# A decoder layer in split fp32: the convolution's sum in PSUM, its gelu behind the next unit's roundings, the residual spread, and the down projection in chunks of 4, 6, 6 and 6 pairs

## The chip, the cores and the metric

One core of one Trainium2 chip. The metric is the device time of one execution in microseconds (us), the median of several runs. The matmul engine (TensorE) is called PE here, VectorE DVE, ScalarE ACT, GpSimd POOL, and SyncE, which only issues transfers, SP.

## The reference, cut to what matters

One decoder layer over 512 positions with 2048 channels: a mixer of four attention groups, an output projection, a layer norm with a scaled residual, then the gated MLP with a causal convolution of width 3 on its gate half, and a second layer norm. The change touches the MLP and what stands around it; D_FF is 5632, that is 44 tiles of 128 (f = 0 to 43).

```python
def conv_ffn(x, w_up, conv_w, conv_b, w_down):
    S = x.shape[1]
    u, g = jnp.split(x @ w_up, 2, axis=-1)
    gp = jnp.pad(g, ((0, 0), (CONV_WIDTH - 1, 0), (0, 0)))
    gc = conv_b
    for tap in range(CONV_WIDTH):
        gc = gc + conv_w[tap] * gp[:, tap:tap + S]
    return (jax.nn.gelu(gc) * u) @ w_down
...
ffn = conv_ffn(h, ffn_w_up[l], ffn_conv_w[l], ffn_conv_b[l], ffn_w_down[l])
h = layer_norm(DEEPNORM_ALPHA * h + ffn, ln2_g[l], ln2_b[l])
```

## The kernel before, in words

**Products.** Every fp32 operand is split into a high part (rounded to the matmul's fp32r) and a low part (the rest), and a product is three matmuls. Both projections of the MLP are done with seven block products in place of eight. A *unit* is one such set of seven, 84 matmuls of 128x128 by 128x256. The up projection has two units for each f (u = 0, 1), in the order (f,0), (f,1); only the last four stand as (42,1), (43,1), (42,0), (43,0). The down projection has 42 units; they run in chunks of pairs of f tiles (CHUNKS), each chunk over the four column sets q, so that a unit is named (chunk, q, u). Behind them stands a plain part of 96 matmuls (L1230) for the last four pairs of the last column set, with the second layer norm behind it. Matmuls of up are on L963, of down on L1115.

**A unit's weights** are made one unit ahead by weight_operands (L909 to L943), called from next_unit. SP loads two tiles wr. ACT writes the negated raw weights into wl (L925) and the rounded ones into wh (L928). POOL's queue then adds the raw weights onto wl with an accumulating transfer (L926), which leaves the low part; so this transfer waits for ACT's L925. POOL forms four sums S (L934 to L937), and each is split into ws by ACT (L899) and DVE (L900). wh and wl have two buffers each, wr four tiles (two units), S two. The first three block products of a unit use wh and wl, the other four ws.

**What stands behind an f.** When both units of f are done, up_finish reads its four PSUM banks (L995 to L1002), and gated makes the convolution: ACT's first tap into the SBUF tile c (L1010), DVE's other two taps (L1011, L1013), ACT's gelu (L1015), POOL's product with the up half (L1016). Every second f, set_aside forms differences of the pair on POOL (L1031, L1032, L1035, L1036) and writes eight blocks to DRAM (hid). up_residual scales the residual on DVE (L1054, L1055) for f = 2 to 17, one of 16 tiles behind each, from a load that it issues itself.

**Down.** hidden_operands loads a pair's blocks from DRAM (hx, hxt) and splits them on ACT and DVE; pairs 0 to 3 are called for in the middle of the last units of up, pairs 4 and 5 at the first unit of down, later ones six pairs ahead, in the last column set of a chunk, as its slots come free. down_add adds a finished set's seven banks into acc (L1128) and down_blocks ends a column set; the banks are those of up (three of group g, five of group a).

**What sets the order.** The code is recorded in program order, and a scheduler places each instruction by data dependence and by priority: weight_operands runs at a priority 900 places ahead, so that its rows move up past the work that stands before it in the code; splits of pairs below SLOTS run 10 ahead and later pairs' 150 behind. Each engine then runs its own row strictly in order.

## Time and profile before

| | us |
|---|---|
| median of 3 runs (lowest, highest) | 2334.61 (2327.23, 2335.04) |
| the profiled execution | 2341.35 |
| its span, first to last instruction | 2339.6 |
| PE busy | 2232.7 (95%) |
| granted clock of PE, mean | 0.983 |

The span has a mixer (to about 900 us), the up projection (917.56 to 1829.44 on PE without its first f), the down projection's units (1829.44 to 2291.86), and the plain part with the layer norm (to 2339.58). In the profile, a row of a timeline gives start, duration, engine, line, operation, result<-operands, count, and in brackets how long the engine had been idle before it and what ended that. A row of waits gives the sum of such idle times, how many, and the longest. The granted clock is 1.00 where TensorE runs at 2.4 GHz and 0.5 where it runs at 1.2 GHz.

### The profile page before, as it was taken

The page shows a single profiled execution, that of the slowest core. Times are in us where ns is not written, and L with a number is a line of the kernel's source. Part 1 is how long each engine was busy: PE and PEld are TensorE (multiplying, and loading weights), DVE is VectorE, ACT ScalarE, POOL GpSimd, SP SyncE. Part 2 cuts the span into 40 slices and gives each one's busy share as a digit, 9 for nine tenths or more (in the row PEclk, how much of TensorE's full clock was granted, in tenths as well). Part 3 has the DMA queues.
Part 4 walks back from the last instruction along what each step waited for, and adds up shares of the span by engine and source line. Part 5 has one row for each costly group of instructions (what it writes and reads, how often), then busy time and mean ns, then how long its engine had stood idle before and what let it go on. Part 6 is the DMA issues. An engine that isn't in the chain of part 4 may idle for free. (4 is left out here: it accounts for less than half of the span.)

```text
span 2339.6 us, 40306 instructions
## 1 busy us (share of the span) xinstructions
PE 2232.7 (95%) x15454; PEld 2083.5 (89%) x15454; DVE 1591.7 (68%) x2204; ACT 1229.5 (53%) x2129; POOL 1368.4 (58%) x1197
## 2 busy tenths in 40 slices
PE   7999999999999998899999999999999899999995
PEld 6788888888888878899999999999999899899994
DVE  7544455456675348687787767777676878677778
ACT  5444453355563135565555555565555666565651
POOL 5212110123234517787887878877777687777874
PEclk9999999999999999999999999999999999999998
DMA  6322223222124363888888777777778888788873
GB/s 228 92 81 73 78 67 106 84 64 62 59 88 149 104 188 94 224 226 227 231 222 238 202 210 207 201 204 197 212 202 227 243 241 233 193 229 216 207 191 115
DMA packets 125362, 392.75 MB, mean 168 GB/s; under 512 B 13632, under 2 KB 23744, under 8 KB 125168
## 3 DMA queue, kind: packets, MB, share of 16 engines
q1 hardware_dynamic: 106304, 287.72, 35.6%
q0 software_dynamic: 18720, 102.24, 24.6%
q8 instruction: 121, 1.98, 0.3%
q14 instruction: 73, 0.60, 0.1%
q10 hardware_dynamic: 144, 0.21, 0.0%
HBM read 354.36 MB, written 35.65 MB: 167 GB/s over the span
## 5 line engine op out<-in xcount | busy, mean ns | idle before, releaser
L900 DVE TENSOR_TENSOR ws<-S,ws 128x512 fp32r<-128x512 f32 x512 | 600.1, 1192 | 244.3 <-ACT ws L899 238.9
L963 PE MATMUL up<-xt,ws 128*128 128x256 f32 x3096 | 386.4, 283 | 0.3 <-DVE ws L900 0.3
L963 PEld LDWEIGHTS up<-xt,ws 128*128 128x128 f32 x3096 | 378.0, 192 | 0.6 <-DVE ws L900 0.6
L899 ACT CAST ws<-S 128x512 fp32r<-128x512 f32 x512 | 307.0, 615 | 114.9 <-POOL S L934 33.5
L100 DVE TENSOR_TENSOR wl<-wr,wh 128x1024 fp32r<-128x1024 f32 x122 | 155.2, 1272 | 213.3 <-ACT wh L99 198.4
L936 POOL TENSOR_TENSOR S<-wr 128x512 f32<-128x512 f32 x128 | 212.0, 1656 | 92.5 <-DVE ws L900 87.3
L342 POOL TENSOR_SCALAR P<-P,r 128x128 f32<-128x128 f32 (+3 forms) x144 | 81.1, 582 | 308.5 <-DVE r L337 166.2
L963 PE MATMUL up<-x,wh 128*128 128x256 f32 x1376 | 258.8, 288 | 0.0
L99 ACT CAST wh<-wr 128x1024 fp32r<-128x1024 f32 x122 | 128.0, 1049 | 233.7 <-PE op L733 78.8
L934 POOL TENSOR_TENSOR S<-wr 128x512 f32<-128x512 f32 x128 | 183.8, 1436 | 108.0 <-issue 45.3
L925 ACT ACTIVATE wl<-wr 128x512 fp32r<-128x512 f32 (+1 forms) x260 | 205.1, 836 | 67.3 <-PE dn L1115 43.5
L928 ACT CAST wh<-wr 128x512 fp32r<-128x512 f32 (+1 forms) x260 | 211.5, 829 | 35.7 <-PE up L963 33.8
L963 PE MATMUL up<-x,wl 128*128 128x256 f32 x688 | 200.8, 292 | 29.5 <-DMA wl<-in_wup_dram 29.3
L963 PEld LDWEIGHTS up<-x,wh 128*128 128x128 f32 x1376 | 220.5, 197 | 0.0
L937 POOL TENSOR_TENSOR S<-wr,S 128x512 f32<-128x512 f32 x128 | 211.8, 1655 | 0.0
L935 POOL TENSOR_TENSOR S<-S,wr 128x512 f32<-128x512 f32 x128 | 198.5, 1551 | 9.7
L1115 PE MATMUL dn<-wh,hx 128*128 128x256 f32 x792 | 157.5, 292 | 13.3 <-DVE acc L1128 8.6
L963 PEld LDWEIGHTS up<-x,wl 128*128 128x128 f32 x688 | 135.8, 197 | 33.7 <-DMA wl<-in_wup_dram 33.7
L1115 PEld LDWEIGHTS dn<-wh,hx 128*128 128x128 f32 x792 | 132.3, 200 | 14.9 <-issue 6.3
L733 PE MATMUL op<-wh,oTs 128*128 128x512 f32 x448 | 140.6, 391 | 0.0
L963 PE MATMUL up<-x,ws 128*128 128x256 f32 x1032 | 137.9, 283 | 0.0
L1015 ACT ACTIVATE c<-c 128x512 f32<-128x512 f32 x44 | 27.8, 632 | 208.0 <-DVE c L1013 208.0
(327 smaller groups left out, 5321.3 us busy)
## 6 DMA issues: line engine op xcount, KB each, us to landing
wr<-in_wup_dram SPq DMA_DIRECT2D x176, 512.0 KB
wl<-in_wup_dram POOLq DMA_DIRECT2D x88, 768.0 KB, 7.5
wr<-in_wm_dram SPq DMA_DIRECT2D x84, 512.0 KB
wr<-in_wdown_dram SPq DMA_DIRECT2D x84, 512.0 KB
wl<-in_wdown_dram POOLq DMA_DIRECT2D x42, 768.0 KB, 7.4
wr<-in_wout_dram SPq DMA_DIRECT2D x32, 512.0 KB
hid<-c SPq DMA_DIRECT2D x44, 256.0 KB
hid<-ht SPq DMA_DIRECT2D x44, 256.0 KB
```

The source lines that it names most:

```text
L100: nc.vector.tensor_sub(l[:, :cols], raw[:, :cols], h[:, :cols].bitcast(F32))
L733: nc.tensor.matmul(ps, ot[ct][:, a, t * P:(t + 1) * P], w[b][:, c2 * 512:(c2 + 1) * 512], start=(first and (a, b) == (0, 0)), stop=(last a ...
L899: self.nc.scalar.copy(h, raw)
L900: self.nc.vector.tensor_sub(l, raw, h.bitcast(F32))
L925: nc.scalar.mul(l3[:, o], i, -1.0)
L928: nc.scalar.copy(h3[:, o], i)
L934: nc.gpsimd.tensor_add(s12[:, 0], a21, a22)
L935: nc.gpsimd.tensor_sub(s12[:, 1], s12[:, 0], a11)
L936: nc.gpsimd.tensor_sub(s34[:, 0], a11, a21)
L937: nc.gpsimd.tensor_sub(s34[:, 1], a12, s12[:, 1])
L963: self.nc.tensor.matmul(ps, w[iw][i][:, k * P:(k + 1) * P], x[j][ix], start=(opens and k == 0 and (i, j) == (0, 0)), stop=(last and k == 3 ...
L1115: self.nc.tensor.matmul(bk[i][:, a * 256:(a + 1) * 256], x[ix][j][:, a * P:(a + 1) * P], w[iw][p][:, q * 256:(q + 1) * 256], start=first a ...
```

## The change

- **Convolution.** For f = 1 to 41 the sum c of the taps is kept in the PSUM bank bk[0] of the same f (its up product has been read by then); gelu reads that bank and writes an SBUF tile c. f = 0, 42 and 43 keep an SBUF tile.
- **Gelu later.** The gelu, the product with the up half and set_aside of f = 1 to 41 are put into a list (defer) and recorded when the next unit's weights have been recorded, and the scheduler is told to place them behind the last ACT row of those weights (issue_after, mark).
- **Residual.** One tile at f = 2, 4, ... 32 in place of f = 2 to 17, with the load one tile ahead of its use.
- **Border.** The splits of pairs 0 to 3 are deferred in the same way, by 0, 1, 1 and 2 units; pairs 4 and 5 are called for at unit (0,1,0).
- **Chunks** of 4, 6, 6, 6 pairs in place of 6, 6, 6, 4, all four column sets each, but the last set of the last chunk has one unit. The count of units, of matmuls and of weight loads is as before. There is one set of down_add more (16 for 15). The load of acc is issued at the first unit of a set of chunk 0, and that of the plain part's weights at unit (3,3,0).

```diff
     def split_pair(self, raw, h, l):
-        self.nc.scalar.copy(h, raw)
+        ins = self.nc.scalar.copy(h, raw)
         self.nc.vector.tensor_sub(l, raw, h.bitcast(F32))
+        return ins
+
+    def defer(self, units, work):
+        self.deferred.append((self.unit_no + units, work))
+
+    def run_deferred(self):
+        todo = [w for n, w in self.deferred if n < self.unit_no]
+        self.deferred = [d for d in self.deferred if d[0] >= self.unit_no]
+        with self.tc.issue_after(self.mark.ins):
+            for work in todo:
+                work()
...
         self.unit_no += 1
+        self.run_deferred()
...
-        self.gated(f, g, up)
+        self.gated(f, g, up, bk[0] if f < FT - 2 else None)
...
-        nc.scalar.activation(c, c, AF.Gelu_apprx_tanh)
+        if 0 < f < FT - 2:
+            self.defer(0, lambda: self.activate(f, c, up))
+        else:
+            self.activate(f, c, up)
+
+    def activate(self, f, s, up):
+        nc = self.nc
+        c = self.tmp("c") if 0 < f < FT - 2 else s
+        nc.scalar.activation(c, s, AF.Gelu_apprx_tanh)
         (nc.vector if f == 0 else nc.gpsimd).tensor_mul(c, c, up)
...
-    CHUNKS = ((0, 0, 6), (1, 6, 6), (2, 12, 6), (3, 18, 4))
+    CHUNKS = ((0, 0, 4), (1, 4, 6), (2, 10, 6), (3, 16, 6))
...
+        def split():
+            with self.tc.high_priority(offset=ahead):
+                for raw, h, l in loaded:
+                    self.split_pair(raw, h, l)
+
+        if kp < 4:
+            self.defer((0, 1, 1, 2)[kp], split)
+        else:
+            split()
...
-            if n and 2 <= f < 18:
-                self.up_residual(f - 2)
+            if n and 2 <= f < 34 and f % 2 == 0:
+                self.up_residual(f // 2 - 1)
```

ACT's row behind f = 27, before. c is the convolution's sum, wl and wh belong to unit (29,0), ws to (28,1) and (29,0), pu to f = 28.

```order
L928 CAST wh<-wr 128x1024
L899 CAST ws<-S 128x512 x3
L1010 ACTIVATE c<-g,prm 128x512
L1015 ACTIVATE c<-c 128x512
L928 CAST wh<-wr 128x512
L925 ACTIVATE wl<-wr 128x512
L925 ACTIVATE wl<-wr 128x1024
L899 CAST ws<-S 128x512
L928 CAST wh<-wr 128x1024
L899 CAST ws<-S 128x512 x3
L995 COPY pu<-up 128x256
```

The same place now; up in L1026 and L1039 is the PSUM bank.

```order
L942 CAST wh<-wr 128x1024
L899 CAST ws<-S 128x512 x3
L1026 ACTIVATE up<-g,prm 128x512
L942 CAST wh<-wr 128x512
L939 ACTIVATE wl<-wr 128x512
L939 ACTIVATE wl<-wr 128x1024
L899 CAST ws<-S 128x512
L942 CAST wh<-wr 128x1024
L899 CAST ws<-S 128x512
L1039 ACTIVATE c<-up 128x512
L899 CAST ws<-S 128x512 x2
L1009 COPY pu<-up 128x256
```

The gelu has moved from ahead of the next unit's negations (L925, now L939) to behind six rows of weights.

POOL's row at the same place, before: from the difference that needs only the first of the pair to the next unit's first sum.

```order
L1031 TENSOR_TENSOR ht<-c 128x256
L934 TENSOR_TENSOR S<-wr 128x512
L935 TENSOR_TENSOR S<-S,wr 128x512
L1016 TENSOR_TENSOR c<-c,up 128x512
L1032 TENSOR_TENSOR ht<-c,ht 128x256
L1035 TENSOR_TENSOR ht<-c 128x256
L1036 TENSOR_TENSOR ht<-c,ht 128x256
L926 DMA wl<-in_wup_dram 128x1536
L936 TENSOR_TENSOR S<-wr 128x512
L937 TENSOR_TENSOR S<-wr,S 128x512
```

And now:

```order
L948 TENSOR_TENSOR S<-wr 128x512
L949 TENSOR_TENSOR S<-S,wr 128x512
L940 DMA wl<-in_wup_dram 128x1536
L1055 TENSOR_TENSOR ht<-c 128x256
L1040 TENSOR_TENSOR c<-c,up 128x512
L950 TENSOR_TENSOR S<-wr 128x512
L951 TENSOR_TENSOR S<-wr,S 128x512
L1056 TENSOR_TENSOR ht<-c,ht 128x256
L1059 TENSOR_TENSOR ht<-c 128x256
L1060 TENSOR_TENSOR ht<-c,ht 128x256
```

The accumulating transfer of wl has moved ahead of the product with the up half and of three differences.

DVE's row at the border of up and down, before: from f = 42's reads of its banks (first L996) to f = 43's (second L996); hxt and hx are operands of the first pairs of down, ws those of units (0,0,0) and (0,0,1).

```order
L996 TENSOR_TENSOR pu<-pu,up 128x256
L997 TENSOR_TENSOR g<-pu,up 128x256
L998 TENSOR_TENSOR uu<-pu,up 128x512
L999 TENSOR_TENSOR g<-uu,up 128x256
L1001 TENSOR_TENSOR up<-uu,up 128x256
L1002 TENSOR_TENSOR up<-uu,up 128x256
L900 TENSOR_TENSOR ws<-S,ws 128x512 x2
L1011 SCALAR_TENSOR_TENSOR c<-g,prm,c 128x511
L900 TENSOR_TENSOR ws<-S,ws 128x512
L1013 SCALAR_TENSOR_TENSOR c<-g,prm,c 128x510
L900 TENSOR_TENSOR ws<-S,ws 128x512
L996 TENSOR_TENSOR pu<-pu,up 128x256
```

And now, from the row behind f = 42's last read to f = 43's first:

```order
L900 TENSOR_TENSOR ws<-S,ws 128x512 x2
L900 TENSOR_TENSOR hx<-hx 128x256 x2
L900 TENSOR_TENSOR ws<-S,ws 128x512
L900 TENSOR_TENSOR hxt<-hxt 128x512
L1027 SCALAR_TENSOR_TENSOR c<-g,prm,c 128x511
L900 TENSOR_TENSOR ws<-S,ws 128x512
L900 TENSOR_TENSOR hx<-hx 128x512 x2
L1029 SCALAR_TENSOR_TENSOR c<-g,prm,c 128x510
L900 TENSOR_TENSOR hx<-hx 128x512 x2
L900 TENSOR_TENSOR hxt<-hxt 128x512
L1010 TENSOR_TENSOR pu<-pu,up 128x256
```

Eight splits of pairs 1 and 2 now stand between the two. Before, splits of the first pairs stood ahead of f = 42's reads; now only pair 0's do.

## Rows read from the trace of the kernel before

**Rows 1.** The page's first part: busy time, share of the span and instructions of each engine.

```profile
PE 2232.7 (95%) x15454; PEld 2083.5 (89%) x15454; DVE 1591.7 (68%) x2204; ACT 1229.5 (53%) x2129; POOL 1368.4 (58%) x1197
```

**Rows 2.** PE's waits from 900 to 2340 us: what PE's line waited for, us in total, times, longest.

```profile
PE up L963 <- DMA wl<-in_wup_dram: 29.3, 20, 5.6
PE dn L1115 <- DVE acc L1128: 9.2, 4, 3.7
PE dn L1115 <- DMA wl<-in_wdown_dram: 8.2, 5, 2.1
```

**Rows 3.** Stretches of the span: from:to, its length, PE busy (matmul records), granted clock of PE, share of the DMA engines in use, GB/s. They begin with unit (2,0); unit (2,1); unit (42,0); units (0,0,0), (1,0,0), (2,0,0) and (3,0,0) of down; the plain part.

```profile
939.07:957.60 18.53, 12.60 (x86) 0.82 0.82 214
957.60:1803.08 845.48, 826.10 (x6807) 0.99 0.81 215
1803.08:1829.44 26.36, 21.86 (x170) 0.94 0.96 283
1829.44:1964.72 135.28, 126.85 (x1011) 0.96 0.88 241
1964.72:2096.53 131.81, 124.59 (x1010) 0.96 0.80 208
2096.53:2224.47 127.94, 123.09 (x1010) 0.99 0.82 216
2224.47:2291.86 67.39, 63.26 (x506) 0.97 0.70 182
2291.86:2339.58 47.72, 21.95 (x98) 0.76 0.28 102
```

**Rows 4.** PE's timeline: the first matmuls of units (28,0) and (28,1), and the one of (29,0) that waited.

```profile
1493.15 0.40 PE L963 MATMUL up<-x,wh 128*128 128x256 f32 x2
...
1503.23 0.40 PE L963 MATMUL up<-x,wh 128*128 128x256 f32 x2
...
1515.57 0.38 PE L963 MATMUL up<-x,wl 128*128 128x256 f32 x1 [1.87 <-DMA wl<-in_wup_dram]
```

**Rows 5.** PE's waits from 957.6 to 1803 us, where unit (2,1) begins and (42,0) begins.

```profile
PE up L963 <- DMA wl<-in_wup_dram: 19.3, 18, 4.5
```

**Rows 6.** ACT's timeline behind f = 27 (first tap, gelu, negations for unit (29,0), last ws splits).

```profile
1498.06 0.82 ACT L1010 ACTIVATE c<-g,prm 128x512 f32<-128x512 f32 x1 [4.17 <-DVE g L999]
1502.73 0.63 ACT L1015 ACTIVATE c<-c 128x512 f32<-128x512 f32 x1 [3.85 <-DVE c L1013]
...
1503.77 1.57 ACT L925 ACTIVATE wl<-wr 128x512 fp32r<-128x512 f32 x2
...
1506.71 1.66 ACT L899 CAST ws<-S 128x512 fp32r<-128x512 f32 x3
```

**Rows 7.** POOL's timeline at the same place.

```profile
1500.47 1.62 POOL L935 TENSOR_TENSOR S<-S,wr 128x512 f32<-128x512 f32 x1
1503.44 1.30 POOL L1016 TENSOR_TENSOR c<-c,up 128x512 f32<-128x512 f32 x1 [1.35 <-ACT c L1015]
...
1507.34 0.86 POOL L926 DMA_DIRECT2D wl<-in_wup_dram  x1
```

**Rows 8.** Groups of ACT's instructions from 957 to 1803 us: count, busy us, mean ns of one, idle time just before them and what ended it.

```profile
L1015 ACT ACTIVATE c<-c 128x512 f32<-128x512 f32 x41 | 25.9, 632 | 205.2 <-DVE c L1013 205.2
```

**Rows 9.** Groups of DVE's instructions, the first from 957 to 1803 us (one of the convolution's taps on DVE), the other two from 1830 to 2292 us (dn is a PSUM bank, pc its copy in SBUF).

```profile
L1011 DVE SCALAR_TENSOR_TENSOR c<-g,prm,c 128x511 f32<-128x511 f32 x40 | 67.3, 1681 | 0.0
...
L1128 DVE TENSOR_TENSOR acc<-acc,dn 128x512 f32<-128x512 f32 x82 | 53.3, 679 | 13.9 <-POOL acc L1128 9.2 <-DMA acc<-ares 3.0 <-PE dn L1115 1.5
L1128 DVE TENSOR_TENSOR acc<-acc,pc 128x512 f32<-128x512 f32 x28 | 43.4, 1549 | 0.0
```

**Rows 10.** Transfers issued from 957 to 1803 us: result<-source, queue, count, KB each, median us from issue to landing.

```profile
wl<-in_wup_dram POOLq DMA_DIRECT2D x81, 768.0 KB, 7.3
```

**Rows 11.** The border: POOL's issue for unit (42,0), PE's waits in (42,0), (0,0,0) and (0,0,2), and DVE's row that opens f = 42's reads.

```profile
1796.81 0.87 POOL L926 DMA_DIRECT2D wl<-in_wup_dram  x1
...
1807.98 0.58 PE L963 MATMUL up<-x,wl 128*128 128x256 f32 x1 [4.50 <-DMA wl<-in_wup_dram]
1833.25 0.39 PE L1115 MATMUL dn<-wh,hx 128*128 128x256 f32 x1 [2.20 <-DVE g L997]
1858.68 0.39 PE L1115 MATMUL dn<-wh,hx 128*128 128x256 f32 x1 [1.76 <-ACT hx L899]
...
1829.34 3.19 DVE L900 TENSOR_TENSOR hx<-hx 128x512 fp32r<-128x512 f32 x2
1832.46 0.41 DVE L996 TENSOR_TENSOR pu<-pu,up 128x256 f32<-128x256 f32 x1
```

**Rows 12.** Around the change from chunk 0's pairs to chunk 1's: PE at the start and in the first products of unit (1,1,0), and ACT before it.

```profile
2000.53 0.55 PE L1115 MATMUL dn<-wh,hx 128*128 128x256 f32 x1 [3.73 <-DVE acc L1128]
2003.15 0.58 PE L1115 MATMUL dn<-wl,hx 128*128 128x256 f32 x1 [2.06 <-DMA wl<-in_wdown_dram]
...
1996.64 0.62 ACT L899 CAST hx<-hx 128x512 fp32r<-128x512 f32 x1 [6.59 <-DMA hx<-hid]
```

**Rows 13.** The end of down: PE at unit (3,2,0), ACT at the plain part's weights, DVE's first row of the plain part.

```profile
2272.14 0.58 PE L1115 MATMUL dn<-wh,hx 128*128 128x256 f32 x1 [2.91 <-DVE acc L1128]
...
2269.55 1.14 ACT L113 CAST wres<-wr 128x512 fp32r<-128x512 f32 x2 [10.87 <-DMA wr<-in_wtail_dram]
...
2303.32 0.67 DVE L1233 TENSOR_TENSOR acc<-acc,dt 128x512 f32<-128x512 f32 x1
```

More of the change, by code (lines that the diff above doesn't have):

```diff
@@ L63, in __init__ @@
         self.every, self.count = 24, 0
-        self.late = deque()
+        self.late, self.deferred = deque(), []
         self.ahead = 0
@@ L773, in out_proj @@
                                    + [self.wdown[q, u] for c, k0, nk in self.CHUNKS
-                                      for q in self.column_sets(c)
-                                      for u in range(k0 // 2, (k0 + nk) // 2)])
+                                      for q in range(4)
+                                      for u in self.set_units(c, q, k0, nk)])
                 self.next_unit()
@@ L930, in weight_operands @@
                 w = [self.tmp("w21", dt=F32R, tag="w") for _ in range(2)]
-                self.split_pair(a21, *w)
+                self.mark = self.split_pair(a21, *w)
                 return [[h3[:, i], l3[:, i]] for i in range(3)] + [w]
@@ L941, in weight_operands @@
                     ws.append([self.tmp("ws", dt=F32R, tag="w") for _ in range(2)])
-                    self.split_pair(t[:, i], *ws[-1])
+                    self.mark = self.split_pair(t[:, i], *ws[-1])
         return [[h3[:, i], l3[:, i]] for i in range(3)] + ws
@@ L1002, in up_finish, with gated @@
         nc.vector.tensor_add(up[:, 256:], uu[:, 1], bk[2][:, :256])
-        self.gated(f, g, up)
-    def gated(self, f, g, up):
+        self.gated(f, g, up, bk[0] if f < FT - 2 else None)
+    def gated(self, f, g, up, c=None):
         nc = self.nc
-        c = self.tmp("c")
+        if c is None:
+            c = self.tmp("c")
         cw = lambda k: self.prm[:, C_CW + 44 * k + f:C_CW + 44 * k + f + 1]
@@ L1048, in up_residual, with load @@
         nc = self.nc
+        def load(i):
+            n, t = divmod(i, NT)
+            gb = (self.bc_row(2, n, "g1"), self.bc_row(3, n, "b1")) if t == 0 else None
+            a = self.tmp("res")
+            nc.sync.dma_start(a, self.res[t][n])
+            return a, gb
         n, t = divmod(i, NT)
-        if t == 0:
-            self.gb1 = self.bc_row(2, n, "g1"), self.bc_row(3, n, "b1")
-        a = self.tmp("res")
-        nc.sync.dma_start(a, self.res[t][n])
+        a, gb = self.res_next if i else load(i)
+        self.gb1 = gb or self.gb1
         nc.vector.scalar_tensor_tensor(a, a, ALPHA, self.gb1[0], op0=ALU.mult, op1=ALU.mult)
@@ L1057, in up_residual, with set_units @@
         nc.sync.dma_start(self.res[t][n], a)
-    CHUNKS = ((0, 0, 6), (1, 6, 6), (2, 12, 6), (3, 18, 4))
+        if i + 1 < 4 * NT:
+            self.res_next = load(i + 1)
+    CHUNKS = ((0, 0, 4), (1, 4, 6), (2, 10, 6), (3, 16, 6))
     @staticmethod
-    def column_sets(c):
-        return range(4 if c < 3 else 3)
+    def set_units(c, q, k0, nk):
+        return range(k0 // 2, (k0 + nk) // 2 if (c, q) != (3, 3) else k0 // 2 + 1)
     SLOTS = 6
@@ L1078, in hidden_operands @@
         loaded = []
-        ahead = 10 if kp < self.SLOTS else -150
+        ahead = 10 if kp < 4 else -150
         def load(h, l, src):
@@ L1105, in hidden_operands @@
             ops += [[h[:, k] for h in xt[i]] for k in range(2)]
-        with self.tc.high_priority(offset=ahead):
-            for raw, h, l in loaded:
-                self.split_pair(raw, h, l)
         self.ho[kp] = ops + b12
+        def split():
[6 more added lines that the diff above has]
+            split()
     def down_product(self, bk, w, i, q, x, first, last):
@@ L1180, in ffn @@
                 self.gated(f, *self.up_first())
-            if n and 2 <= f < 18:
-                self.up_residual(f - 2)
+            if n and 2 <= f < 34 and f % 2 == 0:
+                self.up_residual(f // 2 - 1)
         self.st2 = [self.cst.tile([P, 4, 6], F32, name=f"st2_{t}") for t in range(NT)]
-        self.due = deque((4, 5))
+        self.due = deque()
         acc = []
@@ L1187, in ffn @@
         for c, k0, nk in self.CHUNKS:
-            sets = self.column_sets(c)
-            for q in sets:
+            for q in range(4):
                 bk = [self.bank("g" if i < 3 else "a", "dn") for i in range(7)]
-                nu = nk // 2
+                nu = len(self.set_units(c, q, k0, nk))
                 for u in range(nu):
@@ L1194, in ffn @@
                     self.step_aside()
-                    if c == 0 and u == nu - 1:
+                    if c == 0 and u == 0:
                         acc.append([self.pT.tile([P, 2, 512], F32, tag="T", name="acc")
@@ L1200, in ffn @@
                             nc.sync.dma_start(token(t, q)[:, :cols], self.res[t][q][:, :cols])
+                    if (c, q, u) == (0, 1, 0):
+                        self.due.extend((4, 5))
+                    if (c, q) == (3, 3):
+                        tail = [w for f in range(2) for w in self.load_halves(self.wtail[f])]
                     while self.due:
@@ L1208, in ffn @@
                             self.down_add(i, acc[q], bk[i], c == 0)
-                    if q == sets[-1]:
+                    if q == 3:
                         for kp in (k0 + 2 * u, k0 + 2 * u + 1):
@@ L1213, in ffn @@
                                 self.due.append(kp)
-                        if c == 3 and u == 0:
-                            tail = [w for f in range(2) for w in self.load_halves(self.wtail[f])]
-                if c == 3 or (c, q) == (2, 3):
+                if c == 3:
                     self.down_blocks(q, acc[q])
```

## The prediction

> **What bounds the kernel now.** The page's first part shows PE busy for 95% of the span [rows 1], so only the rest of PE's time, and what a slower granted clock costs behind a wait, can be won. I then read PE's waits: three lines carry most of them, the accumulating transfer of wl in up with 29.3 us, banks that DVE's L1128 hands back late with 9.2, and the same transfer in down with 8.2 [rows 2]. The stretches tell where. A unit that waits for nothing takes 10.08 us (1493.15 to 1503.23) [rows 4], so each stretch has its count of units times 10.08, and an excess [rows 3]: up from (2,1) on, 81 units, 845.48 - 816.48 = 29.0; (42,0) and (43,0) 26.36 - 20.16 = 6.2; chunk 0 of down, 12 units, 135.28 - 120.96 = 14.3; chunk 1 10.85; chunk 2 7.0; chunk 3, 6 units, 6.9. Unit (2,0) has 8.45, at a place that the change leaves as it is. Of up's 29.0, 19.3 are 18 waits for the transfer, none over 4.5 [rows 5]; the rest is the clock, granted at 0.99 over this stretch [rows 3], so about 1% of 845.
>
> How a wait in up comes about is seen behind f = 27. ACT makes the first tap at 1498.06, then its queue stands at the gelu, 3.85 us idle for DVE's taps; the negations for unit (29,0) come behind it, to 1505.3 [rows 6]. POOL stands likewise at the product with the up half, makes three differences, and issues the transfer at 1507.34 [rows 7]. PE takes the result at 1515.57, 1.87 late [rows 4]: 8.2 us from issue, beside a median of 7.3 [rows 10].
>
> **Convolution, gelu, and the residual: up.** What is removed from the path is ACT's idle time before the gelu (205.2 us in 41 times, 5.0 each) and the gelu itself, 0.63 [rows 8], and on POOL the product, 1.30, and three differences, which fill 1504.7 to 1507.3 [rows 7]. The order shows the negations right behind the first tap and the transfer right behind the sum that ended at 1502.1 [rows 7]. The first tap ends at 1498.9; a rounding and negations of 1.57 behind it end near 1501 [rows 6], so the sum decides: issue at 1502.1 in place of 1507.34, 5.2 us earlier. With 8.2 us to landing wl is there at 1510.4, and PE wants it at 1513.7. Since no wait was longer than 4.5, all 18 go. I leave 3 of the 29.0 for transfers that land later than usual; the bounds are 0 (nothing late) and 12 (18 waits shortened by 5.2 only in part, because SP's loads go on sharing the DMA engines, busy 0.81 of this stretch [rows 3]). **Gain 26, from 17 to 29.**
>
> The taps in PSUM change DVE's time, not PE's. The taps on SBUF operands take 1.68 us; the trace has no such tap with its sum in PSUM. Nearest are adds of the same size, 0.68 with one operand in a bank and 1.55 with the copy in SBUF [rows 9]. I take 0.7 to 1.0 each, from 0.68 to 1.7 as bounds: DVE gets some 40 x 2 x 0.8 = 64 us back, beside PE, worth 0 by itself. The residual's 16 tiles have the same instructions; loaded one ahead, DVE no longer stands for them. That work lies beside PE's units; without that cover its two operations, priced like the taps at 0.7 to 1.7 each [rows 9], would be 1.4 to 3.4 a tile.
>
> The landing of 7.3 to 8.2 us is the number on which this hangs [rows 4, 7, 10]. The Trainium skill (DMA: Bandwidth & Descriptors, section Anatomy of one DMA — SWDGE (gpsimd) path) gives 2.0 us and bytes / 436e3 for such a transfer, an estimate of 3.8 us for 768 KB. By that, wl issued at 1507.34 would have landed ahead of PE, up and (42,0) would have had no wait, and 32.2 of the sum would fall away: 2323 in place of 2291. The trace does not agree (8.2), and the measurement decides.
>
> **Border of up and down.** Unit (42,0) waited 4.50 for a transfer issued at 1796.81 [rows 11], 11.2 before it arrived, behind the same gelu and differences of f = 41. Issued 5 us earlier it is in time even at 11.2: 6.2 goes to 0 (0 to 4 stays). In chunk 0 PE waits for f = 42's banks, which DVE reads only from 1832.46, after splits of the first pairs (3.19 for two of them), and at (0,0,2) for ACT's split of an operand [rows 11]. Now f = 42's reads stand ahead of the splits of pairs 1 to 3, so the first wait goes. New is that pair 1's splits stand behind four ws splits and a tap, and pair 1 is wanted within a microsecond of (0,0,0)'s start, at 1829.44; and that pair 3's are ordered in the same way at (0,0,1). Counting DVE's rows of the order from f = 42's reads at 0.7 to 1.6 each, pair 1 is ready 2 to 4 us late. Two such waits of 3, and as much again for the clock behind them as half their length: 9 in place of 14.3. Bounds: 3 (DVE gets there in time) and 18 (both 6 late). The same splits queue ahead of f = 43's bank reads, which (0,0,0) wants for its sixth product; a start 3 late covers that. The loads of hx stay where they were on SP, and acc's loads come earlier, with a whole set's time to spare. **Gain 6.2 + 5.3 = 11.5, from -1.5 to 17.5.**
>
> **Chunks.** The two changes of chunk with six pairs to exchange cost what chunks 1 and 2 have in excess, 10.85 and 7.0: ACT's row reaches a split whose load is still behind SP's weight loads (6.59 us), so ws and wl come late, and the bank of the next set too [rows 12]. The change with four pairs lies in chunk 3 and costs at most the 4.0 that its 6.9 has beside the wait of 2.91 [rows 3, 13]. Now again two changes have six pairs, one stretch later each, and one has four, two pairs being called for earlier at leisure. So I expect 18 for the two of six pairs, as before, and nothing new for the one of four: **gain 0, from -11 to 5** (each of six pairs at 14.5, or at 6.5). One more set of down_add is six adds of 0.68 and two of 1.55 on DVE [rows 9], 7.2 us, in a stage where DVE has room beside PE: 0.
>
> **End.** At (3,2,0) PE waited 2.91 because ACT had stood 10.87 for the plain part's weights, with a bank's copy behind them [rows 13]. Those loads now belong to (3,3,0), the last unit, so nothing but the plain part waits for them: chunk 3's 6.9 becomes 3.4 (0.5 to 7). DVE reached the plain part's first add at 2303.32, 11.5 us after the last of down's units, since the statistics of column set 2 and its blocks stood there [rows 3, 13]. They now fall a unit earlier; four statistics of 0.6 to 0.7 make 2.5 (0 to 4). **Gain 6, from 0 to 10.**
>
> **The sum.** 26 + 11.5 + 0 + 6 = 43.5. The profiled execution took 2341.35 (its span 2339.6 and 1.8 around it), so 2297.9 for it. It lies 6.7 above the median of the runs, so 2334.61 - 43.5 = **2291**.
>
> **The rivals.**
> (a) *Down gives back what up gains.* Border at 15, the changes of chunk at 29, chunk 3 at 5: 26 + 6.2 - 0.7 - 11 + 2 + 2.5 = 25, **2310**. For it: ACT stands 6.59 at a split already [rows 12], and the late splits go ahead of nothing but are wanted at once. Against it: most of the order of the six-pair changes is the same as before.
> (b) *The earlier transfer lands no earlier.* It would run beside SP's two loads for a unit, and the DMA engines are busy 0.81 [rows 3]. Then up keeps about half, 15 of 29, and (42,0) 3: 14 + 3.2 + 5.3 + 6 = 28.5, **2306**. Against it: the median of 7.3 holds at the same load [rows 10]. The Trainium skill (DMA: Bandwidth & Descriptors, section Issuing engines are not separate DMA queues) says that transfers of SP and POOL run on the same DMA engines and interleave; it speaks for this rival, and the (42,0) row, 11.2 us beside SP's extra loads, agrees with it [rows 11].
> (c) *Slower: the bank is held.* bk[0] of f is now free only after the gelu, and f + 2 writes it with its first product, 20.16 us after f's last matmul. The gelu stands behind ws splits that ended 15.2 us after f's last matmul with 5 us of idle ahead of them (1508.4 - 1493.15) [rows 4, 6], so I expect it at 11 to 12. It decides from 20.2 us on: each microsecond beyond is paid by 41 f. Two late on each are 82, **2373**; it is slower than before from some 1.1 late. Against it are those 8 us of slack.
> (d) *It doesn't do what it says:* the gelu is recorded later but reaches ACT's row in the old place. The order excludes that for the place; what can still be is that the transfer waits for the sum L935 of a later time. That is (b)'s time.
>
> **How the numbers follow.** Forecast, 2279 to 2303: 0.55. More than that, below 2279 (border near 3, up near 0): 0.07. (a) 0.18, (b) 0.12, (a) and (b) together, about 2324, 0.03, (c) 0.05. A difference within 0.5%, 11.7 us, is about what a measurement here can't tell from none; it is the range 2323 to 2346. A quarter of (a) and (b) and all of their sum fall there: 0.10. Slower is (c): 0.05. Faster is the rest, 0.85. The range 2277 to 2314 leaves out (c), the sum of (a) and (b), the tail of (a), and the lowest few per cent.
>
> **What would show it.** Right, if PE's wait for wl in up falls from 19.3 to under 5 and POOL issues the transfer near 9 us after the last f's end in place of 14; if ACT's idle time before the gelu falls from 205 to under 40; if the two taps take under 1 us each; if no PE wait in up names the gelu; if (0,0,0) and (0,0,1) wait for splits (hx) rather than for bank reads; if chunks 1 and 2 still have excesses of 7 to 11 with hx and acc as their names. Wrong, if wl is still waited for at odd f, if PE waits for the gelu, or if a change of chunk costs over 15.

## The result and the profile after

| | before | changed |
|---|---|---|
| median of 4 runs each, us (lowest, highest) | 2333.44 (2327.23, 2335.04) | 2306.91 (2301.35, 2309.40) |
| ratio, 95% interval | | 0.988 (0.986 to 0.990) |
| profiled execution, us | 2341.35 | 2307.26 |
| its span, us | 2339.6 | 2305.2 |

Faster by 26.5 us (1.1%; the ratio 0.988 is 1.2%), inside the range of 2277 to 2314, and 16 us slower than the 2291 that was forecast. Between the two profiled executions the gain is 34.1, since the one of before lay 8 us above the median of its runs and the one of the changed kernel at it.

Stretches of the changed kernel, with the columns of [rows 3]: unit (2,0); units (2,1) to (17,1); (18,0) to (43,1); (42,0) and (43,0); the four chunks of down, with 8, 12, 12 and 10 units now.

```profile
938.35:956.65 18.30, 12.90 (x87) 0.81 0.90 229
956.65:1269.13 312.48, 312.48 (x2607) 1.00 0.88 229
1269.13:1774.87 505.74, 504.75 (x4203) 1.00 0.85 218
1774.87:1795.03 20.16, 20.16 (x171) 1.00 1.05 315
1795.03:1893.66 98.63, 88.03 (x674) 0.93 0.86 240
1893.66:2021.76 128.10, 123.67 (x1008) 0.99 0.83 215
2021.76:2147.72 125.96, 123.18 (x1010) 0.99 0.85 223
2147.72:2258.44 110.72, 103.28 (x842) 0.98 0.76 198
```

Up's second row is 31 units of 10.08 us with nothing lost, the third 50 units and 1.74. Taking the count of units times 10.08 from each length:

| excess, us | before [rows 3] | changed | forecast |
|---|---|---|---|
| (2,0) | 8.45 | 8.22 | untouched |
| up, 81 units | 29.0 | 1.74 | 3 |
| (42,0), (43,0) | 6.2 | 0.0 | 0 |
| chunk 0 | 14.3 | 18.0 | 9 |
| chunks 1, 2 | 17.8 | 12.1 | 18 |
| chunk 3 | 6.9 | 9.9 | 3.4 |
| plain part to the end, length | 47.7 | 46.8 | 45.2 |

So up and the two units behind it gave 33.5 of the 34.1, and down gave nothing: 40.0 of excess for 39.0.

PE's waits of the changed kernel from 900 to 2340 us; they answer to [rows 2].

```profile
PE dn L1154 <- DMA wl<-in_wdown_dram: 8.7, 7, 2.2
PE up L977 <- DMA wl<-in_wup_dram: 6.3, 4, 5.3
PE dn L1154 <- DVE acc L1167: 5.9, 3, 3.4
PE dn L1154 <- ACT acc L1177: 4.1, 1, 4.1
PE dn L1154 <- DVE hx L900: 3.8, 2, 2.2
```

Of the 6.3 for wl in up, 5.3 is unit (2,0), so 1.0 is left where [rows 5] had 19.3. POOL's and ACT's timelines behind f = 27, which ends at 1472.04, where PE begins unit (28,0):

```profile
1481.20 1.29 POOL L949 TENSOR_TENSOR S<-S,wr 128x512 f32<-128x512 f32 x1
1482.43 0.88 POOL L940 DMA_DIRECT2D wl<-in_wup_dram  x1
1483.04 1.04 POOL L1055 TENSOR_TENSOR ht<-c 128x256 f32<-128x256 f32 x1
1483.74 1.58 POOL L1040 TENSOR_TENSOR c<-c,up 128x512 f32<-128x512 f32 x1
```

```profile
1477.94 1.58 ACT L939 ACTIVATE wl<-wr 128x512 fp32r<-128x512 f32 x2
...
1481.57 0.60 ACT L1039 ACTIVATE c<-up 128x512 f32<-128x512 f32 x1
```

The transfer leaves 10.4 us after f's end, where it left 14.2 [rows 4, 7], and the sum L949 sets it, as the forecast had it. The gelu comes 9.5 us after f's end and waits for nothing. Over the whole of up it waits 2.0 us where [rows 8] had 205.2, and the median landing of wl is 7.3 us as in [rows 10]. ACT's group of the gelu, and the transfers of wl, from 957 to 1775 us:

```profile
L1039 ACT ACTIVATE c<-up 128x512 f32<-128x512 f32 x40 | 23.5, 588 | 2.0 <-DVE up L1029 1.8
...
wl<-in_wup_dram POOLq DMA_DIRECT2D x82, 768.0 KB, 7.3
```

Groups of DVE's instructions from 957 to 1775 us, the taps and the residual's first step:

```profile
L1029 DVE SCALAR_TENSOR_TENSOR up<-g,prm,up 128x510 f32<-128x510 f32 x40 | 30.1, 753 | 1.3
L1027 DVE SCALAR_TENSOR_TENSOR up<-g,prm,up 128x511 f32<-128x511 f32 x40 | 29.7, 743 | 0.0
...
L1084 DVE SCALAR_TENSOR_TENSOR res<-res,g 128x512 f32<-128x512 f32 x16 | 14.5, 908 | 73.6 <-DMA res<-res 73.6
```

The taps fell from 1.68 and 1.63 to 0.74 and 0.75. DVE still stands 73.6 us for the residual's loads, though each load is recorded one tile ahead.

In down, PE's timeline at units (0,0,0), (0,0,1), (0,3,0) and (3,3,0), and ACT's rows ahead of the last two:

```profile
1797.76 0.39 PE L1154 MATMUL dn<-wh,hx 128*128 128x256 f32 x1 [0.77 <-ACT hx L899]
1801.21 0.80 PE L1154 MATMUL dn<-wh,hx 128*128 128x256 f32 x2 [2.24 <-DVE hx L900]
1816.77 0.51 PE L1154 MATMUL dn<-wh,hx 128*128 128x256 f32 x2 [1.55 <-DVE hx L900]
1820.14 0.50 PE L1154 MATMUL dn<-wh,hxt 128*128 128x256 f32 x2 [1.79 <-DVE hxt L900]
1871.68 0.39 PE L1154 MATMUL dn<-wh,hx 128*128 128x256 f32 x1 [4.09 <-ACT acc L1177]
2246.80 0.35 PE L1154 MATMUL dn<-wh,hx 128*128 128x256 f32 x1 [3.38 <-DVE acc L1167]
```

```profile
1869.55 0.40 ACT L899 CAST hx<-hx 128x256 fp32r<-128x256 f32 x1 [8.40 <-DMA hx<-hid]
1871.05 0.58 ACT L1177 COPY acc<-dn 128x512 f32<-128x512 f32 x1 [1.09 <-DVE acc L1167]
...
2235.03 1.14 ACT L113 CAST wres<-wr 128x512 fp32r<-128x512 f32 x2 [10.79 <-DMA wr<-in_wtail_dram]
```

At the border PE no longer waits for f = 42's bank but for splits, 3.0 at (0,0,0) and 3.3 at (0,0,1). At (0,3,0) it waits for a bank that ACT should have copied, and ACT had stood 8.40 at a split of pair 4 or 5, whose load SP had issued behind seven loads of acc. At (3,3,0) ACT's 10.8 for the plain part's weights is back, one set later than in [rows 13].

### The profile page after: what moved, and what is told of

It is laid out like the page before. It is cut to its first block, busy times and chain, and to the rows that moved or that the text cites. A ratio compares the mean times of both kernels' runs of the same rounds, so it can differ in the third digit from the quotient of the medians.

```text
span 2305.2 us, 40383 instructions
## 1 busy us (share of the span) xinstructions
PE 2222.3 (96%) x15454; PEld 2075.7 (90%) x15454; DVE 1549.5 (67%) x2212; ACT 1234.9 (54%) x2131; POOL 1337.1 (58%) x1199
## 5 line engine op out<-in xcount | busy, mean ns | idle before, releaser
L900 DVE TENSOR_TENSOR ws<-S,ws 128x512 fp32r<-128x512 f32 x512 | 621.5, 1233 | 245.6 <-ACT ws L899 242.3
L899 ACT CAST ws<-S 128x512 fp32r<-128x512 f32 x512 | 314.2, 614 | 140.2 <-PE up L977 57.9
L950 POOL TENSOR_TENSOR S<-wr 128x512 f32<-128x512 f32 x128 | 203.1, 1587 | 111.7 <-DVE ws L900 106.2
L977 PE MATMUL up<-x,wh 128*128 128x256 f32 x1376 | 253.4, 284 | 0.0
L948 POOL TENSOR_TENSOR S<-wr 128x512 f32<-128x512 f32 x128 | 178.7, 1396 | 112.1 <-issue 68.4
L939 ACT ACTIVATE wl<-wr 128x512 fp32r<-128x512 f32 (+1 forms) x260 | 205.3, 837 | 66.8 <-PE dn L1154 55.6
L949 POOL TENSOR_TENSOR S<-S,wr 128x512 f32<-128x512 f32 x128 | 186.8, 1459 | 9.8
L1154 PE MATMUL dn<-ws,hx 128*128 128x256 f32 x1044 | 134.1, 285 | 0.1
```

The lines of the kernel that those rows point to most:

```text
L899: ins = self.nc.scalar.copy(h, raw)
L900: self.nc.vector.tensor_sub(l, raw, h.bitcast(F32))
L939: nc.scalar.mul(l3[:, o], i, -1.0)
L948: nc.gpsimd.tensor_add(s12[:, 0], a21, a22)
L949: nc.gpsimd.tensor_sub(s12[:, 1], s12[:, 0], a11)
L950: nc.gpsimd.tensor_sub(s34[:, 0], a11, a21)
```

## The experiments

The first theory is that of the forecast: the gelu's place in ACT's row, and the product's and differences' place in POOL's, set when wl is sent for, and the sum's place in PSUM is worth nothing to PE. The rivals are the length of DVE's taps and the residual's loads. The first three kernels take up's parts one by one, the next two split up from down. Ratios are to the kernel before, run beside it. Excess below is that of up's 81 units unless another is named, and it is read from one profiled execution of a kernel, which lay up to 9 us from the median of its runs. The *first unit* of an f is (f,0), the *second* (f,1). A unit's *lead* is the time from POOL's issue of its wl to its first matmul; in the kernel before, every unit of up with over 0.3 us of excess has a lead of 8.2 us or less, so that is where a wait may appear.

### Gelu later, alone

```diff
-        nc.scalar.activation(c, c, AF.Gelu_apprx_tanh)
+        if 0 < f < FT - 2:
+            self.defer(0, lambda: self.activate(f, c, up))
+        else:
+            self.activate(f, c, up)
```

> The kernel before with the gelu, the product and the differences of f = 1 to 41 recorded behind the next unit's weights, and nothing else: the convolution's sum stays in SBUF, its taps at 1.65 us each. Theory (the gelu's place in ACT's row sets when the transfer of wl is issued): the stretch from (2,1) to (42,0) falls from an excess of 29.0 us to 0 to 5, the wait for wl there from 19.3 to under 3, the issue behind an odd f from 14.2 us after the last f's end to about 9, unit (42,0) loses its 6.2, and the time falls by 25 to 33 us (ratio 0.986 to 0.989). Rival 1 (the length of the taps matters): the gelu is still late, the product and differences hold POOL, and the excess stays over 12. Rival 2 (waits for the residual's loads): the part of the excess in f = 2 to 17, 18.6 us, stays.

Measured: 2342.96 us median, ratio 1.003 (1.001 to 1.006): no gain. Its stretches (2,1) to (17,1) and (18,0) to (43,1):

```profile
959.97:1301.84 341.87, 322.34 (x2606) 0.98 0.83 219
1301.84:1807.66 505.82, 504.26 (x4202) 1.00 0.84 212
```

Where the residual runs, 31 units, the excess is 29.4, against 18.6 before; where it doesn't, 50 units, 1.8 against 10.4. For the first units of odd f from 19 on the mean lead grew from 7.2 to 12.8, as the first theory says; but for the second units of f = 3 to 17 it fell from 10.5 to 7.0. Moving the gelu moves the wait to the next unit there. (42,0) and (43,0), expected to lose their 6.2, have 10.4. The first theory falls for the kernel as a whole.

### The sum in PSUM, alone

```diff
-        self.gated(f, g, up)
+        self.gated(f, g, up, bk[0] if 0 < f < FT - 2 else None)
```

> The kernel before with the convolution's sum in the PSUM bank for f = 1 to 41, gelu where it was. Theory (place): taps of about 0.75 us in place of 1.65 bring gelu, negations and the transfer 1.8 us earlier, not 5.2; the waits above 1.8 us keep their rest, 2.7, 1.1 and 0.1, and the clock behind them, so an excess of 6 to 14 stays of 29.0, and (42,0) keeps 2 to 5 of its 6.2; time down by 15 to 24 us (ratio 0.990 to 0.994). Rival 1 (taps are all): excess under 4, time down by 27 or more. Rival 2: excess of f = 2 to 17 stays at 18.

Measured: 2305.14 us median, ratio 0.987 (0.984 to 0.990): as fast as the whole change. The same two stretches:

```profile
958.20:1272.79 314.59, 313.21 (x2606) 1.00 0.90 239
1272.79:1778.30 505.51, 504.25 (x4203) 1.00 0.79 211
```

Excess 2.1 and 1.5, so 3.6 for 29.0. The mean lead of the first units of odd f grew by 1.6 (f = 3 to 17, to 7.9) and 2.2 (from 19 on, to 9.4), about the 1.8 by which the two taps shortened; the rest that the expectation gave to larger waits went as well. This is the rival's number.

Up is not all of the gain. (42,0) and (43,0) have 1.7 for 6.2, and the four chunks of down, where no edit was made and the order of ACT's, DVE's, POOL's and SP's rows is the same as before, have 29.4 for 39.0:

```profile
1800.16:1937.17 137.01, 127.64 (x1010) 0.96 0.86 236
1937.17:2061.60 124.43, 121.70 (x1010) 1.00 0.85 221
2061.60:2185.66 124.06, 121.45 (x1011) 1.00 0.85 223
2185.66:2252.88 67.22, 62.21 (x507) 1.00 0.70 182
```

What took those 10 us from down is open.

### The residual spread, alone

```diff
-            if n and 2 <= f < 18:
-                self.up_residual(f - 2)
+            if n and 2 <= f < 34 and f % 2 == 0:
+                self.up_residual(f // 2 - 1)
```

> The kernel before with only the residual spread to f = 2, 4, ... 32 and loaded one ahead. Theory (place): the waits at odd f stay, only the largest of those beside the residual, 4.5 at f = 9 and 2.9 at f = 17, may shrink: excess of 29.0 falls to 18 to 29, time down by 0 to 11 us. Rival 2 (the residual's loads make the waits): excess of f = 2 to 17 falls from 18.6 to under 4, that of all to 12 or less, time down by 16 us or more.

Measured: 2337.95 us median, ratio 1.002 (1.000 to 1.003). The two stretches' excess is 14.4 and 26.3, together 40.7 for 29.0; of the second, 18.8 stand at f = 19 to 29, where the residual now runs, and 7.4 at f = 35 to 41, where it doesn't. The residual takes part in the waits without being all of them, and spreading it by itself saves none of up's. The time stayed all the same, because (42,0) and (43,0) have 1.2 here and down, unedited, 25.7.

### Up as changed, down as before

This kernel is the changed one with CHUNKS, hidden_operands, the loads of acc and of the plain part's weights of before.

> The changed kernel with the down part of before: chunks of 6, 6, 6, 4, splits of pairs 0 to 3 at once, pairs 4 and 5 and the loads of acc and of the plain part's weights where they were. Theory (the whole gain is up's, the down part gave nothing): up's excess 1 to 3, the down stretch's excess about 39 as in the kernel before, and the time that of the changed kernel within 4 us, ratio to before 0.986 to 0.991. Rival (the border and the chunks carry a gain or a loss of their own that chance in one profiled execution hides): ratio under 0.985 or over 0.993.

Measured: 2316.81 us median, ratio 0.991 (0.989 to 0.994), at the upper end of the theory's range and by the medians slower than the changed kernel, though the two intervals overlap a little. Up's excess is 5.0, down's 41.2, but (42,0) and (43,0) have 10.1, where both before and changed have less: the first product of (0,0,0) waits 9.9 for ACT's bank copy L1009, and ahead of that ACT stood 8.1 for an hx load, at a split which the old border queues there. The same wait, 10.2, is the 10.4 of "gelu later"; with the old border and the gelu in its old place (the sum in PSUM alone) it doesn't come. So the border's edit pays for what the deferral costs there.

### Down as changed, up as before

The reverse: the kernel before with defer, and the changed down part.

> The kernel before with only the down part of the change: chunks of 4, 6, 6, 6, the deferred splits of pairs 0 to 3, pairs 4 and 5 at (0,1,0), the loads of acc and of the plain part's weights moved; up as before. Theory (the down part gives nothing by itself, its border and its chunks 18 and 22 us of excess as in the changed kernel): the down stretch's excess 36 to 44, ratio 0.998 to 1.006. Rival (it is a gain that up's changes use up): down's excess under 32, ratio under 0.996.

Measured: 2343.77 us median, ratio 1.004 (1.003 to 1.006): by itself the down part is a small loss. Down's excess is 42.6 and up's 29.4.

### The changed kernel with the sum in SBUF

```diff
-        self.gated(f, g, up, bk[0] if f < FT - 2 else None)
+        self.gated(f, g, up, None)
```

> The changed kernel with the convolution's sum back in SBUF; gelu behind the roundings, residual spread, down as changed. First theory (the gelu's place is what counts, the sum's place is worth nothing to PE): up's excess stays under 5 and the time within 5 us of the changed kernel, 2302 to 2312. New theory (DVE's time counts: with taps of 1.65 and a residual tile it frees the S buffers too late for the second unit of an f): transfers for u = 0 still leave 11 to 13 us ahead of their unit, those for u = 1 of even f up to 32 only 5 to 8, up's excess there 15 to 35 and under 3 from f = 34 on; time 2325 to 2345.

The new theory written there: what is scarce in up is DVE's time, and the bank gives it back. Measured: 2318.08 us median, ratio 0.993 (0.991 to 0.996), faster than the 2325 to 2345 of the new theory and slower than the 2302 to 2312 of the first. The excess is 17.8, within the bounds, every unit of it over 0.1 us at f = 30 or earlier, where the residual runs. At f = 24 to 26 the way is seen. PE's, DVE's and POOL's timelines, and SP's issue of the residual's load:

```profile
1441.14 1.45 PE L977 MATMUL up<-xt,ws 128*128 128x256 f32 x10 [2.58 <-DVE ws L900]
...
1429.90 1.66 DVE L1029 SCALAR_TENSOR_TENSOR c<-g,prm,c 128x510 f32<-128x510 f32 x1
1439.79 0.69 DVE L1084 SCALAR_TENSOR_TENSOR res<-res,g 128x512 f32<-128x512 f32 x1 [8.23 <-DMA res<-res]
...
1442.37 1.67 POOL L950 TENSOR_TENSOR S<-wr 128x512 f32<-128x512 f32 x1 [8.72 <-DVE ws L900]
...
1428.78 0.44 SPq L1078 DMA_DIRECT2D res<-res  x1
```

SP sends for the tile at 1428.78, behind wr loads that wait for POOL's sums; it lands 11 us later; DVE stands there with ws behind it; POOL waits 8.72 for the buffers S that these ws free; so the next wr loads are late too. The row order on DVE has the residual at the same place in the changed kernel, where it waited 9.16 for the same tile and PE lost nothing: there the wait ended 4.9 us into unit (25,1), here 9.3.

### The changed kernel with the gelu at once

```diff
-        if 0 < f < FT - 2:
-            self.defer(0, lambda: self.activate(f, c, up))
-        else:
-            self.activate(f, c, up)
+        self.activate(f, c, up)
```

> The changed kernel with gelu, product and differences recorded at once, ahead of the next unit's roundings as before; the sum stays in PSUM, the residual spread, down as changed. First theory (place): issue for u = 0 behind odd f about 7 to 8 us ahead of its unit, excess of up 12 or more, time 2318 or more. New theory (DVE's time): leads of 8 to 10 us there, enough, excess of up 1 to 6, time within 5 us of the changed kernel.

Measured: 2317.01 us median, ratio 0.993 (0.991 to 0.996). Up's excess is 5.6, with mean leads of 7.8 and 8.6 at the first units of odd f (3 to 17, from 19 on), about as the new theory has it; the deferral takes 3.8 us more of up's excess. The time is 5 us beyond the expectation, and 5.3 us more than in the changed kernel stand in chunk 0, 23.3 for 18.0.

### Three places in down

```diff
-        if kp < 4:
-            self.defer((0, 1, 1, 2)[kp], split)
+        if kp < 6:
+            self.defer((0, 0, 1, 1, 2, 2)[kp], split)
...
-                        tail = [w for f in range(2) for w in self.load_halves(self.wtail[f])]
+                        with self.tc.issue_after(self.mark.ins):
+                            tail = [w for f in range(2)
+                                    for w in self.load_halves(self.wtail[f])]
```

> The changed kernel with three edits in down: splits of pairs 1 and 3 one unit earlier (delays 0, 0, 1, 1), splits of pairs 4 and 5 two units later than their loads, and the plain part's loads behind the last unit's weights on ACT. If the waits of the changed kernel are where its trace puts them: the 6.3 us for hx and hxt in (0,0,0) and (0,0,1) fall under 3 and the clock behind them goes with them (11.9 to under 5), the 4.1 us for ACT's bank copy at (0,3,0) and the 3.4 for DVE's add at (3,3,0) go to 0: down's excess from 40 to 18 to 24, time 2286 to 2296. Rival (the splits only change the place at which ACT or DVE stands): the excess stays over 32, time over 2300.

Measured: 2307.34 us median, ratio 0.990 (0.987 to 0.993): nothing gained on the changed kernel. All three waits went, and others came:

```profile
1797.96 0.38 PE L1154 MATMUL dn<-wh,hx 128*128 128x256 f32 x1 [2.01 <-DVE g L1011]
...
1812.68 2.93 PE L1154 MATMUL dn<-ws,hx 128*128 128x256 f32 x12 [7.00 <-DVE g L1011]
```

With the splits earlier PE waits for f = 42's and 43's banks again, as before the change. Chunk 0's excess fell from 18.0 to 13.8 and chunk 3's from 9.9 to 7.1; chunk 1's grew from 7.1 to 11.6, chunk 2's from 5.0 to 7.0, and the plain part, which now waits for its weights, from 46.8 to 49.6. Down's excess is 39.5 for 40.0. The rival of that expectation holds: these edits choose where ACT and DVE stand.

### Up as changed but f = 40 and 41, down as before

```diff
-        if 0 < f < FT - 2:
+        if 0 < f < FT - 4:
             self.defer(0, lambda: self.activate(f, c, up))
```

and the plain part's weights behind the last unit's, as in the run above.

> The up part of the change (sum in PSUM, gelu behind the roundings, residual spread) with the gelu of f = 40 and 41 recorded at once, the down part of the kernel before, and the plain part's first weights placed behind the last unit's weights on ACT. Theory (up's part is the gain, the down part of the change costs 8 to 10 us, and the 10 us that the two deferred gelus cost at the border go with them): up's excess under 3, (42,0) and (43,0) under 3, down's excess 22 to 30 (that of unit (3,2,0), 4.8, gone), time 2288 to 2298. Rival (the border's waits come from the earlier state of DVE and ACT, whoever's gelu): border again 8 to 12 us worse, time 2303 or more.

Measured: 2301.58 us median, ratio 0.985 (0.979 to 0.990). (42,0) and (43,0) have 4.1 in place of 10.1, up 6.6, down 33.6. The direction holds, the sizes don't: all four miss the theory's bounds, and (3,2,0) keeps 4.2. Nor does the rival's: the border is no longer worse than before. The interval covers the changed kernel's ratio.

### Long taps in PSUM

```diff
+        if s is not None:
+            for n in range(4):
+                nc.vector.scalar_tensor_tensor(self.idle, g[:, :256], cw(1), c[:, :256],
+                                               op0=ALU.mult, op1=ALU.add)
```

> The kernel before with the sum in PSUM and four idle operations of 256 columns on DVE between the two taps (they read the bank and write a scratch tile that nothing uses), so that the taps take as long as in SBUF, 3.2 to 3.4 us together, and the gelu comes as late. Theory (the length of DVE's stretch counts): up's excess is back at 14 to 30, transfers for u = 0 behind odd f 6 to 7.5 us ahead of their unit, time 2322 to 2340. Rival (a sum in SBUF slows POOL's sums beside it, and that is what the bank takes away): up's excess stays under 7, time 2301 to 2310.

Measured: 2329.73 us median, ratio 0.997 (0.995 to 1.000). The two stretches:

```profile
958.55:1287.74 329.19, 319.32 (x2606) 0.98 0.86 230
1287.74:1791.74 504.00, 504.00 (x4202) 1.00 0.84 211
```

With four idle operations of 0.48 the excess is 16.7, where the sum in PSUM alone had 3.6; all of it stands beside the residual. (42,0) and (43,0) have 9.2. So a bank as such doesn't do it: with as long a stretch on DVE half of up's gain and most of the time's is gone. The rival, POOL's sums, is not what brings the waits back: POOL's second sum (L935) takes 1.59 us on average before, 1.36 with the sum in PSUM alone and 1.41 here. But the run is no clean repeat of the taps' length. The leads of the first units of odd f did not fall to 6 to 7.5 as expected, they are 9.8 and 13.3: with the longer stretch the scheduler set the gelu behind the next unit's roundings by itself, and the run became one of "gelu later" with a bank, with waits beside the residual and at (43,0) as there.

### The kernel before again

> The kernel before itself, for a second profile. If the down stretch's 39 us of excess was the chance of one execution: down's excess 25 to 35 here, up's 25 to 33. If it is the kernel's: 37 to 41.

One execution: 2347.84 us, with 31.4 of excess in up and 42.9 in down. So the down stretch's 39 was no chance of one execution; but both profiled executions of this kernel are slower than the median of its runs, and of the 6.5 us between them some 6 stand in these two excesses. A run at the median probably has less of both; none was profiled.

### The first units

```diff
+            with self.tc.issue_after(low.ins) if self.unit_no == 4 else nullcontext():
```

(ahead of POOL's four sums; low is the transfer of wl.)

> The kernel of the run with the gelu deferred up to f = 39 and the down part of before, and POOL's four sums for unit (2,0) placed behind that unit's transfer of wl. In the changed kernel POOL issued that transfer at 938.91, behind its own sums, though ACT's negations were done at 934.7, and PE waited 5.31. Theory (POOL's row holds the transfer): issue about 4 us earlier, PE's wait 5.3 falls to 0 to 1.5 and the slower clock behind it goes, unit (2,0) from 8.3 us of excess to under 2, time 2290 to 2300. Rival (the transfers of the first units land late whenever they start): (2,0) keeps over 6, time 2298 to 2306.

Measured: 2305.79 us median, ratio 0.988 (0.985 to 0.990). Unit (2,0) falls from 8.2 in the changed kernel to 2.9 of excess: its transfer left 3.4 us ahead of it (937.78 to 941.20), where it had left 0.6 behind its start, the 4 us expected. But (3,0), which had no wait, has 8.9; POOL issued its transfer at 963.92, 1.3 ahead of it, behind three differences that this build's order sets there. The wait moved by two units. The time is in the rival's range and not in the theory's, and it is no better than that of the kernel with the gelu deferred up to f = 39.

## Why the prediction was right, and where it was not

- **Up, forecast 26 and 6.2, measured 27.3 and 6.2.** The size was right and the reason half wrong. Issue earlier, gelu off ACT's path, no wait for a bank: all as written. But "beside PE, worth 0 by itself", said of the 64 us that DVE gets back, is the step that failed: alone, the sum in PSUM brought 25.4 of the 29.0 (29.0 - 3.6), and gelu and residual without it 11.2 (29.0 - 17.8). That the sum came out has luck in it. Two ways lead to the same lead, and the forecast saw one; the one it saw, taken alone, gains nothing, since beside the residual the wait goes over to the next unit and the old border costs 10.4.
- **What DVE's time is made of.** DVE is busy 630 of up's 845 us before, and 540 of 820 with the sum in PSUM alone. The rest of its time is not free: it stands for the residual's loads, 54 us before and 74 changed, and what frees S stands behind that. The forecast took those waits for gone; a loop of ws, S, wr and the next load runs through them. That loop was shown in one place, with the sum in SBUF; the size of its share elsewhere is argued from where the excess lies (up to f = 19 in "gelu later", to 17 in "long taps", to 30 with the sum in SBUF). The kernels with SBUF taps and the gelu in its old place wait at odd f without a residual too, 10.4 and 15.9 from f = 18 on in the two profiles of before; there the taps stand on the way from g over the gelu to the negations, and the lead grew by what they shortened. Busy time and these waits together don't order the kernels: 684 us with 29.0 of excess before, 730 with 17.8 for the sum in SBUF, 605 with 3.6 for the sum in PSUM alone. It matters where in the row they stand.
- **The residual, "loaded one ahead, DVE no longer stands for them": wrong.** 73.6 us in 15 waits against 54.0 in 16. The load is recorded one ahead, but SP reaches it behind wr loads that wait.
- **Border, forecast 14.3 to 9: the first two units have 11.9, and chunk 0 has 18.0.** Both split waits are there, 3.0 and 3.3 for 3 and 3. The slower clock behind them cost 5.6, not 3. Another 5.9 stand at (0,2,1) and (0,3,0), where the forecast had pairs 4 and 5 "called for earlier at leisure" and acc's loads "with a whole set's time to spare": SP issued the ones behind the others, and ACT's in-order row stood 8.40.
- **Chunks, forecast 18 for the six-pair changes.** Chunks 1 and 2 have 12.1 in place of 17.8, better by 6; the change into chunk 3 costs some 3 there.
- **End, forecast 3.4 for chunk 3 and 2.5 off the plain part: 9.9 and 0.9.** "Nothing but the plain part waits for them" was wrong: the bank copies of (3,2) stand behind those weights on ACT as (3,1)'s did before, and (3,3,0) waits 3.38 for them.
- **The rivals.** Rival (b) has the nearest number, 2306 for the measured 2306.9, by chance: its mechanism is ruled out, since the median landing stayed at 7.3 and up's wait for wl fell to 1.0. Rival (a), 2310, is right in part: down gave nothing, but with 18.0, 12.1 and 9.9 of excess where it has 15, 29 and 5. Rival (c), the held bank, did not show: the gelu came 9.5 us after f's end with 20 allowed.
- **The signs.** Wait for wl, ACT's idle time before the gelu, the taps' length, no wait for the gelu, and splits at (0,0,0) and (0,0,1): as said. POOL's issue came 10.4 us after f's end, not near 9, and chunks 1 and 2 have 7.1 and 5.0, by waits for wl and acc, not 7 to 11 by hx and acc.
- **The base.** The sum was made against an execution 8 us slower than the median. Between the profiled executions 34.1 of the 43.5 came, and some 7 of those were not in the median to be won.

Open: why the down stretch, with the same order on ACT, DVE, POOL and SP, has 39 to 43 of excess in the kernel before, 29.4 in that with only the sum in PSUM and 25.7 in that with only the residual spread. Its six-pair change at chunk 1 costs 0.5 in the last and 10.9 before; SP sent for the next wr 4 us before unit (1,0,2) began in the one and 2.6 us after in the other. What set that phase was not tried. So a part of down's 40 is how the earlier stages leave the queues, and the loss of 0.4% from the down part alone can't be split among its edits. The kernels with down as changed all have 39.5 to 42.8, so the sum in PSUM alone loses 1.9 us to the changed kernel in up, 1.7 behind it, and wins 10.7 in down. Four kernels here are as fast as the changed one: the sum in PSUM alone, the three places, and the last two with down as before (2301.58 and 2305.79). No interval tells them from it, and the first has by far the smallest edit.

## What to carry to other kernels

An engine that is three quarters busy can still set the pace, when others wait for what stands in its in-order row: follow what is behind its long operations and its waits for loads before calling an edit on it free. When a change has several parts that each move the same wait, run each alone; the part that the diff spends most lines on need not be the one that gains. And look at the stages that an edit doesn't touch: here one of them moved by 10 us and more from kernel to kernel, as much as most of the edits did. In a pipeline whose engines run their rows in order, moving a late split or load ahead of another mostly chooses who stands, so look for what shortens the row.

## What the runs showed of the hardware

Beside a busy POOL the sum's place in a bank halves a tap: 1.68 us on average with all tensors in SBUF [rows 9], 0.74 with the sum in a bank. The Trainium skill (VectorE: DVE Perf Modes, section The TRN2 errata — SBUF-src ops pay a fixed extra latency per instruction) gives a PSUM source the larger fixed cost, 120 cycles against 58; here the operation with the bank is the shorter one, by 0.9 us beside POOL, and as long without it.

What the difference is made of shows in the changed kernel at f = 42, whose sum stays in SBUF: two taps of nearly one size, 0.74 with POOL idle and 1.76 beside POOL's sum. In the up stretches of the six profiles with the sum in SBUF twelve taps had no POOL operation beside them, and they took 0.74 to 0.75. With the sum in a bank POOL makes no difference: in "long taps" 32 taps without POOL took 0.75 on average and 40 beside it 0.74. DVE's and POOL's timelines at f = 42:

```profile
1799.21 0.74 DVE L1027 SCALAR_TENSOR_TENSOR c<-g,prm,c 128x511 f32<-128x511 f32 x1
...
1802.76 1.76 DVE L1029 SCALAR_TENSOR_TENSOR c<-g,prm,c 128x510 f32<-128x510 f32 x1
...
1800.81 1.48 POOL L948 TENSOR_TENSOR S<-wr 128x512 f32<-128x512 f32 x1 [2.67 <-DMA wr<-in_wdown_dram]
1802.36 1.60 POOL L949 TENSOR_TENSOR S<-S,wr 128x512 f32<-128x512 f32 x1
```

The Trainium skill (SBUF — State Buffer, section Who interferes with whom) says that a DVE instruction with two SBUF inputs contends with a GpSimd instruction that reads SBUF; these rows agree with it.
